# One transformer layer on one core: merges as seven products, units in pairs, the second MLP product by 1024 inner features, the output projection by token half, one pool throughout

## The chip, the cores and the metric

One core of one Trainium2 chip runs the whole layer in a single launch. Its engines are TensorE (PE; its weight loads are PEld), VectorE (DVE), ScalarE (ACT), GpSimd (POOL) and SyncE (SP), which issues nearly all DMAs. The metric is the time of one execution in device microseconds, the median of several.

## The reference

One layer over 1024 tokens of width 1024, with 256 context tokens, all in fp32:

```python
hx = modulate(rms_norm(x, norm1), sh1, sc1)                # and hc from ctx
ak, av, gk, gv, lrf, lrb, aq, gq, go, ga, gg = split(hx @ w_in)
attn = softmax(rope(qx) @ [kx, kc].T) @ [vx, vc]           # 8 query heads on 2 key/value heads
gla  = gated linear attention, both directions, 4 heads
y = sigmoid(ga) * (attn @ w_br_attn) + sigmoid(gg) * (gla @ w_br_gla)
x = x + gt1 * (y @ w_out)
x = x + gt2 * (square(relu(modulate(rms_norm(x, norm2), sh2, sc2) @ w_mlp1)) @ w_mlp2)
```

The weights of the two merges and of the output projection are 1024x1024, those of the MLP 1024x4096 and 4096x1024.

## The kernel before

Everything is kept feature-major: 128 features on the partitions, tokens along the free axis, in two halves of 512. Each fp32 operand is split into a rounded high part and a low part (`hilo`, `split`: a cast on ScalarE, a subtraction on VectorE), and every product of a 128x128 weight block with a 128x512 operand block is three matmuls (`mm3`, L167 to L169).

First come the input projections with the gated linear attention (to about 906 us), then softmax attention in 16 blocks of 4 heads x 128 queries, all queries of key/value head 0 and then all of head 1. The results of both branches go to DRAM as high and low parts (`glaT` L768, `atT` L1006). Both stages take their tiles from a pool `sp`, which is closed after attention. Then a second SBUF pool `tl` and a second PSUM pool are opened (L1407) for what follows:

- The merges (`merge_branches` L1137). `operand` loads all of a branch's output, 16 loads of 512 KB; `plain` (L1118) loads 256 columns of weights, splits them into four tiles and makes the four results of 128 features x 512 tokens, each of 8 products. `first` and `second` multiply by the gates.
- The output projection with the same `plain`, in chunks of 256 columns over both token halves. After the last chunk `norm2` normalises half 0, then half 1, and builds the operand blocks of the first MLP product.
- The first MLP product: 16 units of 256 inner features. Each is a 2x2 block product (two halves of the inputs x two column blocks x two token halves) made as seven products for eight (Strassen in Winograd's form): GpSimd makes four sums of weight blocks (`sums`), seven splits follow, and each of the seven results is added up in PSUM and on VectorE. The order is `ORDER` (L1252). The seven operand blocks `B[0..6]` are sums and differences of the normalised activations; only `B[0]` and `B[1]` come from token half 0 alone. The unit stores the seven blocks of its own output (`uD`).
- The second MLP product: 8 chunks of 512 inner features, two column halves each, again seven products; `load` (L1327) brings a block as a raw, a high and a low tile, and L1352 accumulates each result onto the residual in SBUF.

The framework sets the order. It takes the program as written, decides for each engine when an instruction would be ready in its own model of the chip, and lays down a fixed queue for each engine; of what is ready, what is written first goes first. Tiles of one tag are handed out in the order written and wait for a released slot. So a load can be moved forward only as far as a slot is free.

```python
1148:    for c in range(4):                        # merge: 4 chunks of 256 columns
1122:        for s, th in ((0, 0), (1, 0), (0, 1), (1, 1)):
1125:                self.product(p, w[s][h], lambda j: x(4 * h + j, th), 4, h == 0, h == 1, more=False)   # 4 of the 8 products of a result
1359:        for u in (0, 0, 1, 1):                # ahead of the other units:
1360:            next(units[u])                    # products 0 and 1 of two units
```

Of the kernel before, what the change touches and what calls it, by code (L numbers as in the profile page):

```python
# [32 lines left out]
NU, NW, NM = 31, 8, 9  # L33
# [34 lines left out]
class Layer:  # L68
    def __init__(self, ctx, tc, a, out, dbg=None):
        self.ctx, self.tc, self.nc, self.a, self.out = ctx, tc, tc.nc, a, out  # L70
        self.dbg = dbg or {}
        e = ctx.enter_context
        self.cp = e(tc.tile_pool(name="cp", bufs=1))
        self.dp = e(tc.tile_pool(name="dp", bufs=1, space=DRAM))
        self.n = 0

# [11 lines left out]
    def t(self, tag, shape, dt=F32, bufs=2):  # L88
        return self.sp.tile(list(shape), dt, tag=tag, name=self.nm(tag), bufs=bufs)
# [14 lines left out]
    def psum_phase(self, name, bufs):  # L104
        self.pbufs = bufs
        self.ptag = {}
        return self.tc.tile_pool(name=name, bufs=1, space=PSUM)
# [10 lines left out]
    def rsqrt(self, x, n):  # L118
# [8 lines left out]
        for _ in range(5):  # L127
# [617 lines left out]
    def proj_go(self, h):  # L745
# [3 lines left out]
        def g():  # L749
# [5 lines left out]
            def finish():  # L755
                tp, th = pend.pop()
                pt = self.ps("a")
                for f in range(2):
                    for i in range(2):
                        nc.tensor.transpose(pt[:, (2 * f + i) * P:(2 * f + i + 1) * P], th[:, i, f * P:(f + 1) * P], self.ident)  # L760
                for f in range(2):
                    if tp % 2 == 0:
                        gt[f] = (self.m2(F32R), self.m2(F32R))
                    hi, lo = (x[:, (tp % 2) * 256:(tp % 2 + 1) * 256] for x in gt[f])
                    src = pt[:, f * 256:(f + 1) * 256]
                    nc.scalar.activation(hi, src, AF.Copy, scale=self.gnh[:, f:f + 1])
                    nc.vector.scalar_tensor_tensor(lo, src, self.gnh[:, f:f + 1], hi.bitcast(F32), op0=ALU.mult, op1=ALU.subtract)
                    if tp % 2 == 1:  # L768
                        for j in range(2):
                            self.move(self.glaT[j][2 * h + f][:, (tp // 2) * 512:(tp // 2 + 1) * 512], gt[f][j])  # L770
# [15 lines left out]
        return (9, g)  # L786

# [130 lines left out]
    def q_load(self, kv, qb):  # L918
        q = [self.m2(F32R, (P, 4, P)) for _ in range(2)]
# [11 lines left out]
    def attention(self, tail, gate):  # L931

        nc = self.nc
        with self.psum_phase("pat", {"s": 2, "sc": 1, "b": 3}) as self.pp:
# [53 lines left out]
            def values(kv, qb, st, kt):  # L988
# [14 lines left out]
                at = self.S(F32R, (P, 2, 4, P))  # L1003
                self.hilo(at[:, 0], at[:, 1], rv)
                for j in range(2):
# [77 lines left out]
    def U(self, dt=F32R, shape=(P, 2, 512)):  # L1083
        return self.t("U", shape, dt, bufs=NU)

    def m(self, dt=F32, shape=(P, 512)):
        return self.t("m", shape, dt, bufs=NM)
# [7 lines left out]
    def split(self, v, engine=None):  # L1095

        w = self.t("W", (P, 2, 512), F32R, bufs=NW)
        hi, lo = w[:, 0, :], w[:, 1, :]
        if len(v.shape) == 3:
            hi, lo = (x.rearrange("p (a b) -> p a b", b=v.shape[2]) for x in (hi, lo))  # L1100
        elif len(v.shape) == 4:
            hi, lo = (x.rearrange("p (a b c) -> p a b c", b=v.shape[2], c=v.shape[3]) for x in (hi, lo))
        self.nc.scalar.copy(hi, v)  # L1103
        (engine or self.nc.vector).tensor_tensor(lo, v, hi.bitcast(F32), op=ALU.subtract)  # L1104
        return w

    def wcols(self, name, c0):
        return self.a[name][:, c0:c0 + 256].rearrange("(k p) c -> p k c", p=P)

    def product(self, out, w, x, n, first, last, at=lambda j: j * P, more=True):  # L1110

        for j in range(n):
            c = at(j)
            xh, xl = x(j)
# [125 lines left out]
    def plus(self, a, b, o, engine=None):  # L1240
        r = self.m()
        (engine or self.nc.vector).tensor_tensor(r, a, b, op=o)
        return r

# [205 lines left out]
```

## Time and profile before

| | |
|---|---|
| median of 3 runs | 2216.52 us (2214.68 to 2220.52) |
| the profiled execution | 2216.28 us, its span 2214.5 us |
| PE busy | 2038.4 us (92%), 12622 matmuls |
| DVE busy | 1492.8 us (67%) |
| ACT busy | 934.7 us (42%) |
| POOL busy | 449.5 us (20%) |
| DMA | 271.50 MB |

```profile
PE   5999898998989999999998599996899998889999
DVE  6533778669588487877776224438666666778997
POOL 2100322213131022100000000001222333433642
PEclk9999999998999999999999799997999998989999
```

Each digit is the busy share of one fortieth of the span (55.4 us), in tenths. TensorE is nearly always busy; its dents in the second half are slice 23 (1218 to 1273 us), slices 28 and 29 (1495 to 1606) and slices 34 to 36 (1827 to 1993). Matmuls overlap in time in the records, so their own durations (about 390 ns) add up to more than they take; the spacing of their starts is what counts.

### The profile page before, as it was taken

Reading aid. Unit: us, or ns where it says so; the run is one execution under the profiler, and the core shown is the slowest. Engines: PE = TensorE matmul, PEld = TensorE weight load, DVE = VectorE, ACT = ScalarE, POOL = GpSimd, SP = SyncE. Lnnn points to the kernel's source line nnn. Section 1 sums busy time; section 2 is a strip of 40 time slices with the busy share of each in tenths; the row PEclk is TensorE's granted clock in tenths of the full one; section 3 lists DMA queues with packets and bytes.
Section 4 is the critical chain, followed back from the end, with each engine's and each line's share of the span. In section 5 each row is a group of like instructions: output and inputs, shape, how many; then the busy total and the mean of one; then the engine's idle time right before and its main releaser. Section 6 shows DMA issues by size and latency. Waiting matters only on the chain.

```text
span 2214.5 us, 32247 instructions
## 1 busy us (share of the span) xinstructions
PE 2038.4 (92%) x12622; PEld 1718.3 (78%) x12622; DVE 1492.8 (67%) x2372; ACT 934.7 (42%) x1607; POOL 449.5 (20%) x272
## 2 busy tenths in 40 slices
PE   5999898998989999999998599996899998889999
PEld 2898687887878998788887488884688886667877
DVE  6533778669588487877776224438666666778997
ACT  3344544434254322566665111222655554323431
POOL 2100322213131022100000000001222333433642
PEclk9999999998999999999999799997999998989999
DMA  8143421232325333231222915320444446343433
GB/s 292 57 119 110 138 87 45 96 102 72 121 82 172 106 123 134 79 88 54 58 57 65 372 54 204 128 86 34 143 157 152 157 157 214 122 142 117 171 120 118
DMA packets 208696, 271.50 MB, mean 123 GB/s; under 512 B 16880, under 2 KB 144000, under 8 KB 208544
## 3 DMA queue, kind: packets, MB, share of 16 engines
q1 hardware_dynamic: 208480, 269.31, 36.4%
q8 instruction: 99, 1.62, 0.3%
q0 software_dynamic: 64, 0.13, 0.1%
q14 instruction: 53, 0.43, 0.1%
HBM read 191.79 MB, written 77.61 MB: 122 GB/s over the span
## 4 chain that ended last, share of the span: by engine, by line
PE 52%; DVE 12%; DMA 3%; issue 2%; ACT 1%; POOL 1%; SPq 0%; DVEq 0%; POOLq 0%; ACTq 0%
PE g L168 12%; PE g L169 12%; PE g L167 12%; PE b L973 3%; DVE U L1352 2%; PE b L167 2%; PE b L169 2%; PE b L168 2%; DVE W L1104 2%; DMA U<-u 2%; DVE G L848 1%; PE s L167 1%; PE s L169 1%; PE s L168 1%; DVE U L1332 1%
## 5 line engine op out<-in xcount | busy, mean ns | idle before, releaser
L167 PE MATMUL g<-U,W 128*128 128x512 f32 x1280 | 503.5, 397 | 60.7 <-ACT W L1103 30.6
L168 PE MATMUL g<-U,W 128*128 128x512 f32 x1280 | 508.2, 397 | 26.0 <-POOL U L1332 20.7
L169 PE MATMUL g<-U,W 128*128 128x512 f32 x1280 | 505.5, 396 | 0.0
L167 PEld LDWEIGHTS g<-U,W 128*128 128x128 f32 x1280 | 244.3, 191 | 120.5 <-ACT W L1103 34.5
L168 PEld LDWEIGHTS g<-U,W 128*128 128x128 f32 x1280 | 245.5, 192 | 83.1 <-POOL U L1332 23.7
L169 PEld LDWEIGHTS g<-U,W 128*128 128x128 f32 x1280 | 245.6, 192 | 51.7 <-DVE W L1104 0.2
L167 PE MATMUL g<-whi,S 128*128 128x256 f32 x896 | 261.8, 292 | 0.0
L168 PE MATMUL g<-wlo,S 128*128 128x256 f32 x896 | 256.0, 286 | 0.0
L169 PE MATMUL g<-whi,S 128*128 128x256 f32 x896 | 255.5, 285 | 0.0
L1262 POOL TENSOR_TENSOR Q<-R 128x512 f32<-128x512 f32 x32 | 43.0, 1342 | 954.8 <-DMA R<-in_w_mlp_dram 532.8
L1103 ACT CAST W<-R 128x512 fp32r<-128x512 f32 x144 | 89.0, 623 | 321.1 <-PE g L169 285.6
L1352 DVE SCALAR_TENSOR_TENSOR U<-g,mc,U 128x512 f32<-128x512 f32 x224 | 161.7, 742 | 49.8 <-PE g L169 49.6
L1104 DVE TENSOR_TENSOR W<-R,W 128x512 fp32r<-128x512 f32 x144 | 128.6, 897 | 66.4 <-ACT W L1103 65.1
L168 PEld LDWEIGHTS g<-wlo,S 128*128 128x128 f32 x896 | 171.6, 191 | 1.4 <-issue 0.4
L167 PEld LDWEIGHTS g<-whi,S 128*128 128x128 f32 x896 | 171.6, 191 | 1.4
L169 PEld LDWEIGHTS g<-whi,S 128*128 128x128 f32 x896 | 171.3, 191 | 0.3
L1104 DVE TENSOR_TENSOR W<-Q,W 128x512 fp32r<-128x512 f32 x128 | 112.4, 879 | 65.2 <-ACT W L1103 64.7
L167 PE MATMUL g<-S,whi 128*128 128x512 f32 x336 | 139.8, 416 | 5.1 <-ACT S L262 5.1
L1103 ACT CAST W<-Q 128x512 fp32r<-128x512 f32 x128 | 79.0, 621 | 146.3 <-PE g L169 114.3
L169 PE MATMUL g<-S,wlo 128*128 128x512 f32 x336 | 136.5, 406 | 0.0
L168 PE MATMUL g<-S,whi 128*128 128x512 f32 x336 | 135.8, 404 | 0.0
L155 POOL TENSOR_TENSOR wlo<-wraw,whi 128x1024 fp32r<-128x1024 f32 x32 | 89.9, 2827 | 224.3 <-ACT whi L154 221.0
(299 smaller groups left out, 3966.8 us busy)
## 6 DMA issues: line engine op xcount, KB each, us to landing
R<-in_w_mlp_dram SPq DMA_DIRECT2D x32, 1024.0 KB, 5.2
wraw<-in_w_in_dram SPq DMA_DIRECT2D x60, 512.0 KB, 4.3
u<-m SPq DMA_DIRECT2D x112, 256.0 KB, 3.3
U<-u SPq DMA_DIRECT2D x56, 512.0 KB, 6.8
m<-in_w_ada_dram SPq DMA_DIRECT2D x64, 256.0 KB, 4.4
G<-in_w_ada_dram SPq DMA_DIRECT2D x16, 512.0 KB, 10.5
S<-in_xT_dram SPq DMA_DIRECT2D x8, 512.0 KB, 9.8
wraw<-in_w_in_dram SPq DMA_DIRECT2D x16, 256.0 KB, 3.4
```

The source lines that it names most:

```text
L155: self.lo_engine.tensor_tensor(lo[:, s, :], raw, hi[:, s, :].bitcast(F32), op=ALU.subtract)
L167: nc.tensor.matmul(out, lh, rh, start=first, stop=False, skip_group_check=more)
L168: nc.tensor.matmul(out, lh, rl, start=False, stop=False, skip_group_check=more)
L169: nc.tensor.matmul(out, ll, rh, start=False, stop=last, skip_group_check=more)
L848: nc.vector.tensor_tensor(uv[:, :, :, s, :], xv[:, :, :, 1 - s, :], tv[:, :, :, s, :], op=ALU.mult)
L973: nc.tensor.transpose(pt[:, h * P:(h + 1) * P], src, self.ident)
L1103: self.nc.scalar.copy(hi, v)
L1104: (engine or self.nc.vector).tensor_tensor(lo, v, hi.bitcast(F32), op=ALU.subtract)
L1262: tt(s[0], a21, a22, op=ALU.add)
L1332: (nc.gpsimd if i in (2, 3, 6) else nc.vector).tensor_tensor(lo, raw, hi.bitcast(F32), op=ALU.subtract)
L1352: nc.vector.scalar_tensor_tensor(d, p, self.mc[:, 3, b:b + 1], d, op0=ALU.mult, op1=ALU.add)
```

## The change

The merges become units of the same kind as in the MLP: 4 units of 256 columns in each merge, seven products each (`unit`, `merge_unit`); the branch outputs are stored as the seven operand blocks (`glaD`, `atD`), whose differences GpSimd makes (`operands`). Attention runs its blocks in groups of four (both key/value heads, queries q and q + 4), so that a group's four results make one set of operand blocks. Units run in pairs, one product of each in turn (`pair`), and during a pair the blocks for the next stage are loaded step by step (`load_blocks`). The output projection takes the token halves one after the other, with the weights loaded twice. The first MLP product opens with products 0 and 1 of four units. The second goes by 1024 inner features and 256 columns. The pool `sp` stays open to the end: its 19 + 16 tiles of 4 KB hold the operand blocks, the gates, the results and the residual; the weight tiles (`R`, `W`, six in place of eight) take the place of the input projection's weights once these are done. The reciprocal root takes three Newton steps in place of five.

```diff
-        for _ in range(5):
+        for _ in range(3):
...
+                th_ = tp // 2
                 for f in range(2):
...
-                    nc.scalar.activation(hi, src, AF.Copy, scale=self.gnh[:, f:f + 1])
-                    nc.vector.scalar_tensor_tensor(lo, src, self.gnh[:, f:f + 1], hi.bitcast(F32), op0=ALU.mult, op1=ALU.subtract)
...
+                        gt[f, th_] = self.m2()
+                    nc.scalar.activation(gt[f, th_][:, (tp % 2) * 256:(tp % 2 + 1) * 256], pt[:, f * 256:(f + 1) * 256], AF.Copy, scale=self.gnh[:, f:f + 1])
+                if tp % 2 == 1:
+                    self.operands(gt, th_, lambda i: self.glaD[h, i])
...
+    def operands(self, b, th, dst, view=lambda t: t):
+        nc = self.nc
+        tt = nc.gpsimd.tensor_tensor
+        put = lambda i, t: nc.sync.dma_start(dst(i), view(t))
+        if th == 0:
+            put(0, b[0, 0])
+            put(1, b[1, 0])
+            return
+        put(2, b[1, 1])
+        tt(b[0, 0], b[0, 1], b[0, 0], op=ALU.subtract)
+        put(4, b[0, 0])
+        tt(b[0, 1], b[1, 1], b[0, 1], op=ALU.subtract)
+        put(6, b[0, 1])
+        tt(b[1, 1], b[1, 1], b[0, 0], op=ALU.subtract)
+        put(5, b[1, 1])
+        tt(b[1, 0], b[1, 0], b[1, 1], op=ALU.subtract)
+        put(3, b[1, 0])
...
-        q = [self.m2(F32R, (P, 4, P)) for _ in range(2)]
+        t = self.S(F32R, (P, 2, 4, P))
+        q = [t[:, j] for j in range(2)]
...
-                at = self.S(F32R, (P, 2, 4, P))
-                self.hilo(at[:, 0], at[:, 1], rv)
-                for j in range(2):
-                    self.move(self.atT[j][4 * kv:4 * kv + 4, :, qb * P:(qb + 1) * P].rearrange("h d t -> d h t"), at[:, j])
-            blocks = [(kv, qb) for kv in range(2) for qb in range(NT)]
+                th = qb // 4
+                self.at[kv, th] = rb
+                if kv == 1:
+                    if th == 0:
+                        return
+                    t0 = qb % 4 * P
+                    for t in range(2):
+                        self.operands(self.at, t, lambda i: self.atD[:, i, :, t0:t0 + P].rearrange("j d t -> d j t"), lambda r: r.rearrange("p (h t) -> p h t", t=P))
+            blocks = [(kv, q + 4 * th) for q in range(4) for kv in range(2) for th in range(2)]
+            self.at = {}
...
-            self.lo_engine = nc.gpsimd
+            self.close_wts.close()
+            self.wts, self.close_wts = self.open("tw", side="right", reuse_waits="tile")
             late = []
             for n, (kv, qb) in enumerate(blocks):
                 nxt, sg = None, iter(())
-                if n == 4:
+                if n == 0:
                     kvs[1] = self.kv_load(1)
+                if n in (9, 11):
+                    self.load_blocks(self.glaD, n // 11)
                 if n + 1 < len(blocks):
...
+        w = self.t("W", (P, 2, 512), F32R, bufs=6)
+        hi, lo = (w[:, i, :].rearrange("p (a b) -> p a b", b=P) for i in range(2))
...
+    ORDER = (0, 1, 5, 4, 6, 2, 3)
+    def four(self, i):
+        return (self.S if i in (0, 1, 5) else self.G)(F32R, (P, 2, 512))
+    def split_block(self, b, v, engine=None):
+        self.nc.scalar.copy(b[:, 0, :], v)
+        (engine or self.nc.vector).tensor_tensor(b[:, 1, :], v, b[:, 0, :].bitcast(F32), op=ALU.subtract)
+    def load_block(self, b, src, engine=None):
+        v = b[:, 1, :].bitcast(F32)
+        self.nc.sync.dma_start(v, src)
+        self.split_block(b, v, engine)
+        return b
+    def load_blocks(self, src, i):
+        for j in range(4):
+            self.nB[i, j] = self.load_block(self.four(i), src[j, i], self.nc.gpsimd if j % 2 else None)
...
+    def unit(self, src, sink, halves=True):
+        B = self.B
+        raw = self.raw_weights(src)
+        blk = (lambda kh, s: raw[:, kh::2, s * P:(s + 1) * P]) if halves else (lambda kh, s: raw[:, 4 * kh:4 * kh + 4, s * P:(s + 1) * P])
+        A, w, bank = {0: blk(0, 0), 1: blk(1, 0)}, {}, {}
+        for i in self.ORDER:
+            wi = w.pop(i) if i in w else self.split(A[i])
+            if i in (0, 1, 4):
+                bank[i] = self.ps("p" if i == 0 else "g")
+            p = bank[{1: 1, 4: 4, 2: 4}.get(i, 0)]
+            self.product(p, wi, lambda j: B[i, j], i in (0, 1, 4), True)
+            if i == 1:
+                A[4], A[5], A[6], A[2] = self.sums(blk)
+                w[3] = self.split(blk(1, 1))
+            sink(i, p)
+            yield
+    def pair(self, a, b, also=None):
+        for i in self.ORDER:
+            next(a)
+            next(b)
+            if also:
+                also(i)
...
+        def store(k):
+            return lambda b, th, v: nc.sync.dma_start(self.yD[k][b][:, th * 512:(th + 1) * 512], v)
+        for i in self.ORDER[2:]:
+            self.load_blocks(self.glaD, i)
+        self.B, self.nB = self.nB, {}
+        u = lambda c: self.merge_unit("w_br_gla", c, 1, store(0))
+        self.pair(u(0), u(1))
+        self.pair(u(2), u(3), lambda i: self.load_blocks(self.atD, i))
+        self.B, self.nB = self.nB, {}
+        self.Y = Y = {}
+        u = lambda c, last: self.merge_unit("w_br_attn", c, 0, last)
+        self.pair(u(0, store(1)), u(1, store(1)))
+        def keep(b, th, v):
+            Y[b, th] = (self.G if th else self.S)(F32R, (P, 2, 512))
+            self.split_block(Y[b, th], v)
+        def also(i):
+            if i in (0, 4):
+                th = i // 4
+                for b in range(4):
+                    Y[b, th] = self.load_block((self.G if th else self.S)(F32R, (P, 2, 512)), self.yD[1][b][:, th * 512:(th + 1) * 512], nc.gpsimd if b % 2 else None)
+        self.pair(u(2, keep), u(3, keep), also)
...
+        self.B = {}
+        Z = {}
+        for th in range(2):
+            ssq = self.m()
...
+                bank = [self.ps("p") for _ in range(4)]
+                for kh in range(2):
+                    raw = self.raw_weights(self.a["w_out"][kh * 512:(kh + 1) * 512, c * 512:(c + 1) * 512].rearrange("(k p) c -> p k c", p=P))
+                    for i in range(4):
+                        w = self.split(raw[:, :, i * P:(i + 1) * P])
+                        self.product(bank[i], w, lambda j: self.Y[4 * kh + j, th], kh == 0, kh == 1, more=False)
+                        if kh == 0:
+                            continue
+                        b = 4 * c + i
+                        v = Z[th, i % 2, c][:, i // 2, :]
+                        nc.vector.scalar_tensor_tensor(v, bank[i], mc[:, 0, b:b + 1], v, op0=ALU.mult, op1=ALU.add)
...
+            self.norm2(th, ssq, lambda t, e, j: Z[t, e, j // 2][:, j % 2, :])
...
+        for j in range(4):
+            norm(0, j)
+            norm(1, j)
+            tt(z(0, 0, j), z(1, 0, j), z(0, 0, j), op=ALU.subtract)
+            tt(T2(j), z(1, 1, j), z(0, 0, j), op=ALU.subtract)
+            self.block(5, j, T2(j))
...
+            b = 2 * q + s
+            d = x[b][th]
+            nc.vector.scalar_tensor_tensor(d, p, self.mc[:, 3, b:b + 1], d, op0=ALU.mult, op1=ALU.add)
+        return self.unit(self.wcols("w_mlp2", q * 256, n * D), sink)
...
-        for u in (0, 0, 1, 1):
+        for u in (0, 1, 0, 1, 2, 3, 2, 3):
             next(units[u])
-        for g in units:
-            run_all(g)
+        for u in (0, 2):
+            for _ in range(5):
+                next(units[u])
+                next(units[u + 1])
+        for u in range(4, 14, 2):
+            self.pair(units[u], units[u + 1])
+        self.nB = {}
+        load = lambda n: lambda i: self.load_blocks(self.uD[4 * n:4 * n + 4], i)
+        self.pair(units[14], units[15], load(0))
...
+        for n in range(4):
+            self.B, self.nB = self.nB, {}
+            self.pair(self.mlp2_unit(n, 0, x), self.mlp2_unit(n, 1, x))
+            self.pair(self.mlp2_unit(n, 2, x), self.mlp2_unit(n, 3, x), load(n + 1) if n < 3 else None)
...
-        with self.tc.tile_pool(name="sp", bufs=2) as self.sp:
-            self.small_constants()
-            self.attention(*self.in_projection())
-        with self.tc.tile_pool(name="tl", bufs=2, reuse_waits="tile") as self.sp, self.psum_phase("pout", {"g": 6, "a": 2}) as self.pp:
+        self.sp, close_sp = self.open("sp")
+        self.mid, close_mid = self.open("mid")
+        self.wts, self.close_wts = self.open("wts", side="right")
+        self.small_constants()
+        self.attention(*self.in_projection())
+        close_mid.close()
+        self.mid, close_mid = self.open("tm", reuse_waits="tile")
+        with self.psum_phase("pout", {"p": 4, "g": 2, "a": 2}, "tile") as self.pp:
             self.load_mod()
             self.merge_branches()
             self.out_projection()
             self.mlp()
```

## Rows read from the trace of the kernel before

**Rows 1.** Stretches: us, PE, PEld, DVE, ACT, POOL busy (x instructions), clock, DMA, GB/s.
```profile
906.00:1211.00 305.00, 304.47 (x1756) 248.70 (x1754) 231.48 (x469) 208.72 (x444) 1.05 (x1) 1.00 0.23 66
1211.00:1240.80 29.80, 0.00 (x0) 0.00 (x0) 1.38 (x2) 1.26 (x3) 0.00 (x0) 0.55 0.95 359
1240.80:1506.50 265.70, 265.43 (x1165) 218.78 (x1165) 103.97 (x170) 53.64 (x89) 5.09 (x4) 0.99 0.40 143
1506.50:1566.00 59.50, 28.12 (x92) 20.78 (x93) 53.26 (x101) 21.34 (x38) 6.46 (x5) 0.68 0.13 42
1566.00:1852.00 286.00, 286.00 (x1261) 236.23 (x1261) 172.75 (x212) 163.99 (x277) 90.41 (x63) 1.00 0.47 166
1852.00:2211.00 359.00, 325.49 (x1348) 259.66 (x1347) 306.05 (x366) 119.73 (x164) 150.10 (x82) 0.95 0.39 136
```
**Rows 2.** Timeline of TensorE near the end: start, duration, what.
```profile
2201.06 0.39 PE L167 MATMUL g<-U,W 128*128 128x512 f32 x1
...
2210.36 0.39 PE L169 MATMUL g<-U,W 128*128 128x512 f32 x1
```
**Rows 3.** Timeline from attention to the merges; in brackets the idle time before.
```profile
1210.61 0.39 PE L169 MATMUL b<-G,S 128*128 128x512 f32 x1
...
1228.13 0.38 SPq L1092 DMA_DIRECT2D R<-in_w_br_gla_dram  x1
...
1240.16 1.14 ACT L1103 CAST W<-R 128x512 fp32r<-128x512 f32 x2 [27.78 <-DMA R<-in_w_br_gla_dram]
```
**Rows 4.** Timeline of the second half's normalisation.
```profile
1518.12 0.74 DVE L1191 SCALAR_TENSOR_TENSOR U<-g,mc,U 128x512 f32<-128x512 f32 x1
...
1530.35 1.09 PE L366 MATMUL a<-ident,ty 128*128 128x128 f32 x4 [7.97 <-DVE ty L130]
...
1532.10 1.29 DVE L1218 TENSOR_TENSOR U<-U,m 128x512 f32<-128x512 f32 x2 [1.89 <-ACT m L1215]
...
1541.96 1.22 PE L167 MATMUL g<-U,W 128*128 128x512 f32 x2 [10.52 <-ACT U L184]
```
**Rows 5.** Waits of TensorE, 1205 to 2215 us: total, times, longest.
```profile
PE g L167 <- ACT W L1103: 30.6, 2, 29.8
PE g L168 <- POOL U L1332: 20.7, 7, 5.8
```
**Rows 6.** DMA issues of the operand blocks: count, KB each, median us to landing.
```profile
U<-u SPq DMA_DIRECT2D x56, 512.0 KB, 6.8
```
**Rows 7.** Groups by line and shape, 1566 to 1852 us (first MLP product).
```profile
L1104 DVE TENSOR_TENSOR W<-Q,W 128x512 fp32r<-128x512 f32 x60 | 41.5, 692 | 64.2 <-ACT W L1103 63.6
L1104 DVE TENSOR_TENSOR W<-R,W 128x512 fp32r<-128x512 f32 x45 | 39.7, 882 | 0.3 <-ACT W L1103 0.3
...
L1263 POOL TENSOR_TENSOR Q<-Q,R 128x512 f32<-128x512 f32 x16 | 28.0, 1747 | 0.0
...
L1264 POOL TENSOR_TENSOR Q<-R 128x512 f32<-128x512 f32 x16 | 20.8, 1300 | 0.0
```
**Rows 8.** The same view, 1241 to 1418 us (merges).
```profile
L1104 DVE TENSOR_TENSOR W<-R,W 128x512 fp32r<-128x512 f32 x39 | 26.5, 691 | 58.1 <-ACT W L1103 58.0
L1103 ACT CAST W<-R 128x512 fp32r<-128x512 f32 x39 | 23.8, 622 | 136.3 <-PE g L169 132.8 <-DMA R<-in_w_br_gla_dram 3.3
```
**Rows 9.** The same view, 1852 to 2211 us (second MLP product).
```profile
L1352 DVE SCALAR_TENSOR_TENSOR U<-g,mc,U 128x512 f32<-128x512 f32 x224 | 161.7, 742 | 49.8 <-PE g L169 49.6
...
L1104 DVE TENSOR_TENSOR W<-Q,W 128x512 fp32r<-128x512 f32 x60 | 65.5, 1092 | 1.0 <-ACT W L1103 1.0
L1332 POOL TENSOR_TENSOR U<-U,U 128x1024 fp32r<-128x1024 f32 x24 | 62.0, 2589 | 59.2 <-ACT U L1331 59.2
...
L1104 DVE TENSOR_TENSOR W<-R,W 128x512 fp32r<-128x512 f32 x46 | 53.3, 1162 | 0.0
```
**Rows 10.** The same view, 0 to 880 us, VectorE (output of the gated linear attention).
```profile
L767 DVE SCALAR_TENSOR_TENSOR m<-a,gnh,m 128x256 fp32r<-128x256 f32 x32 | 15.3, 479 | 12.5 <-ACT m L766 12.2
```
**Rows 11.** Costliest groups of the whole execution: the casts of weights.
```profile
L1103 ACT CAST W<-R 128x512 fp32r<-128x512 f32 x144 | 89.0, 623 | 321.1 <-PE g L169 285.6
```

More of the change, by code (lines that the diff above doesn't have):

```diff
@@ L1093, in raw_weights, with split @@
         return raw
[L1095 to L1102, printed above, removed]
+    def split(self, v):
+        w = self.t("W", (P, 2, 512), F32R, bufs=6)
+        hi, lo = (w[:, i, :].rearrange("p (a b) -> p a b", b=P) for i in range(2))
@@ L1103, in split @@
         self.nc.scalar.copy(hi, v)
-        (engine or self.nc.vector).tensor_tensor(lo, v, hi.bitcast(F32), op=ALU.subtract)
+        self.nc.vector.tensor_tensor(lo, v, hi.bitcast(F32), op=ALU.subtract)
         return w
[L1107 to L1114, printed above, removed]
-            self.mm3(out, w[:, 0, c:c + P], w[:, 1, c:c + P], xh, xl, first and j == 0, last and j == n - 1, more and not first)
@@ new lines, in product @@
+    def product(self, out, w, x, first, last, more=True):
+        for j in range(4):
+            c, b = j * P, x(j)
+            self.mm3(out, w[:, 0, c:c + P], w[:, 1, c:c + P], b[:, 0, :], b[:, 1, :], first and j == 0, last and j == 3, more and not first)
+    ORDER = (0, 1, 5, 4, 6, 2, 3)
[4 more added lines that the diff above has]
+        (engine or self.nc.vector).tensor_tensor(b[:, 1, :], v, b[:, 0, :].bitcast(F32), op=ALU.subtract)
@@ L1211, in norm2, with block @@
+    def block(self, i, j, v, engine=None):
+        self.B[i, j] = self.four(i)
+        self.split_block(self.B[i, j], v, engine)
+    def norm2(self, th, ssq, z):
         nc, mc = self.nc, self.mc
@@ L1284, in store @@
[L1284 to L1298 removed]
+        tt = nc.vector.tensor_tensor
@@ new lines, in mlp1_unit, with put, act, sink @@
+        X = {}
+        def put(i, v):
+            nc.sync.dma_start(self.uD[u, i], v)
+        def act(v, src, p=None):
+            if p is not None:
+                tt(v, v, p, op=ALU.add)
+            nc.scalar.activation(v, src, AF.Relu)
+            nc.scalar.activation(v, v, AF.Square)
+        def sink(i, p):
+            if i == 0:
+                X[1] = self.S(F32, (P, 2, 512))
+            elif i == 4:
+                X[2] = self.S(F32, (P, 2, 512))
+            x11, x12 = X[1][:, 0, :], X[1][:, 1, :]
+            x22, x21 = (X[2][:, 0, :], X[2][:, 1, :]) if 2 in X else (None, None)
+            if i == 0:
+                nc.scalar.copy(x11, p)
@@ L1299, in mlp1_unit @@
             elif i == 1:
-                done(11, self.plus(keep[11], p, ALU.add))
-                store(0, out[11])
+                act(x11, x11, p)
+                put(0, x11)
             elif i == 5:
-                keep[12] = copied(p)
+                nc.scalar.copy(x12, p)
             elif i == 4:
-                keep[22] = copied(p)
+                nc.scalar.copy(x22, p)
             elif i == 6:
-                done(22, self.plus(keep[22], p, ALU.add))
-                store(2, out[22])
+                act(x22, x22, p)
```

307 lines of the change are left out of this document (126 added, 181 removed).

## The prediction

> **What bounds the kernel now.** I read three views in this order: the busy time of each engine by stage, then who made TensorE wait, then the timeline at each gap. The stage table shows [rows 1] that attention (906 to 1211 us) and the first MLP product (1566 to 1852) keep TensorE busy without a hole, while three stretches do not: 1211 to 1240.8 has no matmul at all, 1506.5 to 1566 has 92, and the second MLP product has 1348 in 359 us. In the last 9.3 us two matmuls 41 places apart start at 2201.06 and 2210.36 [rows 2]: 0.2268 us for each 128x512 matmul at full clock. With that price the table reads as lost time. Stretch 1211 to 1240.8 loses 29.8. Stretch 1506.5 to 1566 loses 59.5 - 92 x 0.2268 = 38.6. The second MLP product loses 359 - 1348 x 0.2268 = 53.3. Merges and output projection lose 265.7 - 1165 x 0.2268 = 1.5, the first MLP product nothing. So the part after attention is 3840 matmuls x 0.2268 = 870.9 us plus about 129 us of the rest: 121.7 of holes, the others being small matmuls of the normalisation and the clock after a hole, and 3.7 us from the last matmul to the end.
>
> What makes the holes: at the start, SyncE issues the 16 loads of the first merge's operand ahead of the first weights; attention's last matmul starts at 1210.61, the weights are issued at 1228.13 and the cast of them begins at 1240.16 [rows 3]. At 1506 to 1566 TensorE has a few products of two units as cover and then waits for the second normalisation, 7.97 us ahead of the transposes and 10.52 for the first new operand block [rows 4]. In the second MLP product it waits for the low parts of the loaded blocks, 20.7 us behind GpSimd alone [rows 5]; those blocks need three tiles each, so the loads run late (6.8 us to landing [rows 6]), and VectorE is busy 306 of 359 us [rows 1].
>
> **The change part by part.** The sum starts from the profiled execution: span 2214.5, time 2216.28, so 1.8 around it; the median of the runs shown is 2216.52, the same within 0.3 us.
>
> *Merges as seven products.* Before: 2 merges x 4 chunks x 32 products x 3 = 768 matmuls. After: 2 x 4 units x 7 x 4 products x 3 = 672. Minus 96, or 21.8 us, on the path, since TensorE is the bound there (rates in [rows 1]). The rest of the 3744 matmuls stays: output projection 384, each MLP product 1344. 3744 x 0.2268 = 849.1 us. This is the surest term.
>
> *What the seven products add.* Weight sums on GpSimd, four a unit, each between 1.30 and 1.75 us [rows 7], some 6 us a unit, where GpSimd had next to no work (5 us in 266 [rows 1]); 56 loads of 256 KB with cast and subtraction in place of the old 32 loads of 512 KB; partial results kept and added on VectorE. A pair of units lasts 168 x 0.2268 = 38.1 us. VectorE in the busiest merge pair (loading the next operand): 14 weight splits, 14 block splits, and per unit 3 adds, 4 multiplications. At the price without GpSimd, 0.69 [rows 8], that is 28 x 0.69 + 14 x 0.69 = 29 us; at the price it has when GpSimd is busy, 1.09 to 1.16 [rows 9], for those with both inputs in SBUF, 28 x 1.12 + 8 x 0.69 + 6 x 1.12 = 44. So between 0 and 6 us are lost in such a pair, more where gates are added: 0 to 23 over the four pairs. I take 5, because only a part of the time has GpSimd at work: the first MLP product, which has the same sums, shows 0.69 and 0.88 mixed [rows 7].
>
> *One pool throughout, loads ahead.* The operand blocks 0 and 1 are loaded during attention blocks 9 and 11, the weight ring is opened as soon as the last input projection is done, and PSUM is handed over tile by tile. So the first 4 products of the pair (10.9 us) have everything when attention ends, and block 5 can take the three to four free tiles during the last attention block. What follows needs 16 blocks of 256 KB, 4 MB; the hole of before carries 359 GB/s [rows 1], so 12 us, begun as the last score tiles come free, against 16.3 us of cover with block 5. The hole of 29.8 falls to between 0 and 29.8; I take 1. If the loads come only when attention has let go of its tiles, the cover ends first and the hole is the old one.
>
> *Attention and what lies before it.* Attention stays at TensorE's pace. Both head groups are loaded at once, the queries move into the big tiles, 16 casts and subtractions go, 16 GpSimd sums and 8 block splits come; all beside a TensorE that is busy 304.5 of 305 us [rows 1]. A cast that stands ahead of attention's own casts and waits for its DMA holds ScalarE some 3 us. The first query tile now holds one of the 19 tiles that the last gate needs, so that gate waits for the first scores. I put -2 to +10 here. Before attention 32 operations of 0.48 us leave VectorE [rows 10] and each reciprocal root loses 6 small operations; the output operand waits for 16 GpSimd sums that nobody waits for. I put -10 to 0. Together -12 to +10, taken as -2.
>
> *Output projection by token half.* The normalisation of half 0 now lies beside 192 matmuls (43.5 us) of half 1: hidden. That of half 1 is exposed, with 8 products (21.8 us) of four units as cover instead of 4. Working: the chain from the last product to the row on all partitions took 1518.12 to 1532.1, 14 us [rows 4]; without 6 of 18 small operations about 12. Then each of four blocks costs VectorE five operations, 3.3 us, and the first needs ScalarE twice in between: first block at 16, last at 26, and some 10 us of weight splits and adds lie on VectorE in the same stretch, so up to 36. TensorE comes for the last block at 24: a wait of 2 to 12. The other end is the hole of now less the added cover, 38.6 - 10.9 = 27. I take 8.
>
> *Second MLP product by 1024.* The VectorE accumulations fall from 224 to 112, at 0.742 [rows 9] 83 us less; blocks are loaded half a chunk (38 us) ahead into tiles that have just come free, against 6.8 us to landing, and each block takes one tile instead of three. VectorE per pair: 14 x 1.12 + 14 x 0.742 = 26 us, with loads up to 42, mean at most 34 of 38.1. So TensorE is the bound, and of 53.3 us between 0 and 53.3 stay; I take 8, with the change from the first product to the second in it, where the residual tiles are loaded last.
>
> *Small rest.* First MLP product 1, the small matmuls of half 0's normalisation 3, clock after a hole 1: where TensorE had stood still 10.5 us it ran at half its clock for some 5 us (granted clock 0.68 in that stretch [rows 1]), and shorter waits should cost less.
>
> Sum: 1211.0 - 2 + 1 + 849.1 + 5 + 8 + 8 + 5 + 3.7 = 2088.8; with 1.8 around it 2090.6, say **2091 us**, 5.7% less.
>
> *A rule that speaks against it.* A weight split takes 0.691 us where GpSimd is idle and 1.09 to 1.16 where it works 150 of 359 us [rows 1, 8, 9]. The Trainium skill ("SBUF — State Buffer", Who interferes with whom) says that a VectorE operation with two SBUF inputs and a GpSimd operation that reads SBUF exclude each other for the whole instruction. By it the two engines' times in the second MLP product would add; that is rival B. The trace agrees as far as it goes: the split of raw weights in the first MLP product, which meets the sums, takes 0.882, and that of the sums 0.692 [rows 7].
>
> **The rivals.**
> *A, the hole at the start stays.* The loads of blocks 4, 6, 2, 3 need tiles that attention holds to its end. For it: ScalarE waited 27.8 us for the loads and the weights behind them [rows 3]. Against: half the bytes are wanted, the weights come early. Time 2091 + 29 = 2120.
> *B, VectorE and GpSimd get in each other's way.* GpSimd works 16 units x 6 + 56 x 1.3 (half of the 2.59 for the double width [rows 9]) = 169 us in the second MLP product, VectorE 168 operations of 0.69 with two SBUF inputs (116 us) and 83 us of accumulations: 368 if nothing overlaps, 305 if the accumulations hide. I price it with the loss of now staying whole, 45 us more than I took (inside the 63 that 368 would cost), and the merges losing 23 instead of 5. Time 2091 + 45 + 18 = 2154.
> *C, slower: the ring of weight slots.* It shrinks from 8 to 6, and two slots in a pair (four at the start of the first MLP product) hold the last weights from the second step on, so four move. If a split could start only when the product before its own has ended, each of 56 + 32 + 224 = 312 products would wait for cast and subtraction, 0.62 + 0.69 = 1.3 us [rows 8]: 406 us, time 2497. It decides from 125/312 = 0.40 us a product. For it: the casts' idle time ends on TensorE, 285.6 us [rows 11], so the ring is already what holds them. Against: they run that far ahead, TensorE waited for weights 30.6 us in all, 29.8 of it at the start [rows 5], and four slots are 10.9 us of products against 1.3.
>
> **How the numbers follow.** Forecast 0.70, its own range 2061 to 2114 (all best ends at once, -12 up to attention's end, 0 at the start, in the merges and in the second product, 2 after the output projection, give 2061). A 0.13, B 0.10, C 0.04, anything else 0.03. All worst ends at once would give 2214, which needs every cover to fail; the range goes from 2056 (5 us more for small matmuls that hide) to one large term staying, 2138. A measurement of this kernel can tell 0.3% (6.6 us) from no change: its three runs lie 5.8 us apart. Faster 0.94 (forecast, A, B and most of the rest), the same 0.02, slower 0.04.
>
> **What would show it.** Right: the first merge matmul within 3 us of attention's last; 672 matmuls in the merges in some 155 us; one short wait after the output projection, below 15 us, with at most a brief loss of clock; the second MLP product in 305 to 320 us with VectorE below nine tenths. Wrong: weight casts behind the block loads at 1211 (A); splits over 1.1 us and VectorE above 95% (B); TensorE waiting for W in every product (C); attention longer than 310 us.

## The result and the profile after

The changed kernel takes 2158.4 us (median; 2154.2 to 2160.3), the kernel before 2218.5 beside it: ratio 0.9725, interval 0.9699 to 0.9751. That is 60 us less, where 125 were forecast; 2158 lies above the range. The profiled execution has a span of 2152.3. One execution of all the runs below was slow, the profiled one of *e10b_stores* (2493 us at a granted clock of 0.75): it is left out of that run's time, and its trace is not read.

Stretches of the changed kernel, columns as in [rows 1]: the passage into attention, attention, merges and output projection, the normalisation of half 1, the two MLP products.

```profile
850.00:950.00 100.00, 79.16 (x417) 63.55 (x416) 61.26 (x116) 41.60 (x87) 11.27 (x9) 0.93 0.61 182
950.00:1214.80 264.80, 264.63 (x1528) 219.45 (x1526) 196.34 (x401) 178.26 (x384) 21.96 (x17) 1.00 0.16 48
1214.80:1490.80 276.00, 262.80 (x1105) 207.80 (x1104) 202.67 (x266) 115.98 (x204) 108.14 (x69) 0.98 0.64 215
1490.80:1527.50 36.70, 14.02 (x53) 10.85 (x52) 34.09 (x42) 23.94 (x40) 13.06 (x8) 0.67 0.08 29
1527.50:1844.10 316.60, 307.73 (x1318) 247.16 (x1316) 189.50 (x236) 177.46 (x308) 117.06 (x78) 0.99 0.49 164
1844.10:2148.10 304.00, 303.96 (x1296) 244.51 (x1296) 223.25 (x255) 110.37 (x186) 151.90 (x99) 0.99 0.43 143
```

The second MLP product is now without a hole, and still 1296 recorded matmuls fill 304 us, 10 more than they would at the price of [rows 2]. The timeline near the end shows why: these two are 40 places apart, 9.33 us, so 0.2333 us each, where [rows 2] has 0.2268.

```profile
2138.54 0.40 PE L174 MATMUL g<-G,W 128*128 128x512 f32 x1
...
2147.87 0.40 PE L175 MATMUL p<-G,W 128*128 128x512 f32 x1
```

The timeline where [rows 3, 4] had the two large holes, and at the passage between the MLP products. The first merge product now stands right behind attention, but two waits follow; at the normalisation TensorE waits once, for 22.68 us.

```profile
1214.56 0.40 PE L175 MATMUL b<-G,S 128*128 128x512 f32 x1
1214.80 0.39 PE L173 MATMUL p<-S,W 128*128 128x512 f32 x1
...
1522.59 0.76 PE L173 MATMUL g<-S,W 128*128 128x512 f32 x1 [22.68 <-DVE S L1382]
...
1835.20 0.50 PE L175 MATMUL g<-S,W 128*128 128x512 f32 x1 [2.57 <-DVE W L1128]
...
1844.14 0.76 PE L173 MATMUL p<-S,W 128*128 128x512 f32 x1 [6.35 <-DVE S L1431]
```

The longest waits of TensorE from 1150 us on, in the columns of [rows 5] (total, times, longest): L1382 is the addition that frees a PSUM bank, L1431 the accumulation of the second product, L1127 and L1128 cast and subtraction of weights.

```profile
PE g L173 <- DVE S L1382: 22.7, 1, 22.7
PE p L173 <- DVE S L1431: 6.3, 1, 6.3
PE g L175 <- DVE W L1128: 6.1, 2, 3.6
PE p L173 <- ACT W L1127: 3.4, 1, 3.4
PE g L173 <- ACT W L1127: 3.1, 1, 3.1
```

*The account.* From the first merge matmul (1214.80) to the last (2147.87) are 933.3 us with its own length; 3744 x 0.2333 are 873.6. What successive starts lie further apart than that, summed by place, is the loss there, the slow clock behind a wait included (e1 to e9 are experiments below; two of their expectations put the start of the merges at 13.2 and 12.6, which this way of counting makes 12.2 and 11.6):

| | forecast | after | e1 | e3 | e6 | e9 |
|---|---|---|---|---|---|---|
| us for a 128x512 matmul | 0.2268 | 0.2333 | 0.2267 | 0.2333 | 0.2267 | 0.2267 |
| start of the merges | 1 | 11.7 | 12.3 | 12.1 | 12.2 | 11.6 |
| rest of merges | 5 | 8.2 | 10.6 | 10.1 | 11.6 | 10.9 |
| normalisation, half 1 | 8 | 25.4 | 26.1 | 10.9 | 12.9 | 11.6 |
| into the second MLP product | 8 | 10.8 | 15.1 | 13.3 | 14.7 | 6.8 |
| first merge matmul at | 1209 | 1214.8 | 1219.9 | 1220.8 | 1208.8 | 1211.6 |

Against the forecast's 2088.8 the changed kernel has more: matmuls 24.5, merges 13.9, normalisation 17.4, passage 2.8, end of attention 5.8, rest -0.9; together 63.5, the whole difference. (The instruction orders of after and e3 are the same up to the merges, yet the first merge matmul comes at 1214.8 and 1220.8: single spans are read to 6 us, the losses by place more closely.)

### The profile page after: what moved, and what is told of

Its sections match the earlier page's. It is cut to its first block, busy times and chain, and to the rows that moved or that the text cites. A ratio compares the mean times of both kernels' runs of the same rounds, so it can differ in the third digit from the quotient of the medians.

```text
span 2152.3 us, 32698 instructions
## 1 busy us (share of the span) xinstructions
PE 2016.5 (94%) x12526; PEld 1688.3 (78%) x12526; DVE 1482.9 (69%) x2216; ACT 1002.8 (47%) x1783; POOL 632.1 (29%) x408
## 4 chain that ended last, share of the span: by engine, by line
PE 47%; DVE 5%; DMA 4%; issue 2%; ACT 1%; POOL 0%; SPq 0%; DVEq 0%; ACTq 0%; POOLq 0%
PE p L173 7%; PE p L175 7%; PE p L174 7%; PE g L173 4%; PE g L175 4%; PE g L174 4%; PE b L996 3%; PE b L173 2%; PE b L175 2%; PE b L174 2%; PE s L173 2%; PE s L174 1%; PE s L175 1%; DVE G L1155 1%; DMA S<-y 1%
## 5 line engine op out<-in xcount | busy, mean ns | idle before, releaser
L1128 DVE TENSOR_TENSOR W<-Q,W 128x512 fp32r<-128x512 f32 x160 | 131.1, 824 | 96.1 <-ACT W L1127 95.8
L173 PE MATMUL p<-S,W 128*128 128x512 f32 x384 | 155.1, 404 | 11.6 <-DVE S L1431 6.3
L1127 ACT CAST W<-R 128x512 fp32r<-128x512 f32 x152 | 93.9, 620 | 151.1 <-PE p L175 106.4
L1128 DVE TENSOR_TENSOR W<-R,W 128x512 fp32r<-128x512 f32 x152 | 138.2, 914 | 24.2 <-ACT W L1127 24.2
L1175 POOL TENSOR_TENSOR Q<-R 128x512 f32<-128x512 f32 x40 | 59.9, 1497 | 323.2 <-DVE W L1128 225.4
L175 PE MATMUL p<-S,W 128*128 128x512 f32 x384 | 154.2, 402 | 0.2 <-DVE W L1128 0.2
L174 PE MATMUL p<-S,W 128*128 128x512 f32 x384 | 154.2, 402 | 0.0
L1127 ACT CAST W<-Q 128x512 fp32r<-128x512 f32 x160 | 98.6, 621 | 118.3 <-PE g L175 53.3
L174 PE MATMUL p<-G,W 128*128 128x512 f32 x384 | 152.0, 396 | 0.0
L173 PE MATMUL p<-G,W 128*128 128x512 f32 x384 | 151.9, 395 | 0.0
L175 PE MATMUL p<-G,W 128*128 128x512 f32 x384 | 151.9, 395 | 0.0
L191 DVE TENSOR_TENSOR G<-b,G 128x512 fp32r<-128x512 f32 x164 | 111.8, 686 | 48.0 <-ACT G L190 47.8
## 6 DMA issues: line engine op xcount, KB each, us to landing
G<-in_w_ada_dram SPq DMA_DIRECT2D x16, 512.0 KB, 10.6
```

Source lines behind the costliest of these rows:

```text
L173: nc.tensor.matmul(out, lh, rh, start=first, stop=False, skip_group_check=more)
L174: nc.tensor.matmul(out, lh, rl, start=False, stop=False, skip_group_check=more)
L175: nc.tensor.matmul(out, ll, rh, start=False, stop=last, skip_group_check=more)
L191: self.nc.vector.tensor_tensor(lo, src, hi.bitcast(F32), op=ALU.subtract)
L1128: self.nc.vector.tensor_tensor(lo, v, hi.bitcast(F32), op=ALU.subtract)
L1175: tt(s[0], a21, a22, op=ALU.add)
```

## The experiments

**The price of a matmul.** A product has two operands in SBUF: the weights, and the moving tile that streams past them. The address of the weight tiles W (read from the built programs; traces hold none) was the one thing that I found to differ for every product of the part after attention: 192 past a multiple of 256 bytes before, 224 after; the moving tiles (U, then S and G) start 192 past one in both. *e1_pad32*, from the changed kernel:

```diff
+        pad = self.pad.tile([P, 8], F32, name="pad", bufs=1)   # own pool, right side, under "wts"/"tw"
```

> The changed kernel with a dead tile of 32 bytes a partition under the pool of the weight tiles, so that each weight tile W starts 32 bytes lower (at a multiple of 64 bytes, 448 past a multiple of 512, where it was 480 past); nothing else. Theory 1 (where the weights lie in SBUF sets the pace): the matmuls after attention start every 0.2267 us again, as in the kernel before, instead of every 0.2333; 3744 x 0.0066 = 24.7 us less, so 2134 us, ratio 0.9886 to the changed kernel. Rival (the slower pace comes from how two products alternate, or from what the other engines do): spacing stays 0.2333 and the time 2158, within 6 us.

2141.7 us, 0.9657 (0.9634 to 0.9680) of before. Theory 1 holds in the pace, 0.2267; of the 24.7 us about 8 went into longer waits at four places (table). *e2_before_w32* does the reverse to the kernel before:

```diff
+            self.shift = self.t("shift", (P, 8), bufs=1)   # ahead of the first W
```

> The kernel before, with a dead tile of 32 bytes a partition ahead of its weight tiles, so that W starts 32 bytes higher (32 past a multiple of 64). Theory 1 (place of the weights): its matmuls after attention go from one every 0.2267 us to one every 0.2333: 3840 x 0.0066 = 25 us more where TensorE is the bound, 2244 us, ratio 1.011 to the kernel before (less where a wait hides it). Rival (pace set by the alternation of products): 0.2267 and 2218 stay, ratio 1.000.

2234.4 us, 1.0072 (1.0053 to 1.0091), and 0.2333: the pace is as forecast, the time 16 of the 25 us. Then which places are good? *p160* and *p224* are e1 with 40 and 56 numbers in the dead tile.

> The changed kernel with a dead tile of 160 bytes: weight tiles at 64 past a multiple of 256 (64 past a multiple of 64: 0). If a start at a multiple of 64 bytes is all that counts: one matmul every 0.2267 us, 2141. If 256 counts (the fast ones so far all start 192 past a multiple of 256, like the moving tiles; the head's weights in the kernel before start 64 past one and were slow): 0.2333, 2158.

2160.7 us.

> The changed kernel with a dead tile of 224 bytes: weight tiles at a multiple of 256 (and of 64). If a multiple of 64 is all that counts: 0.2267 and 2141. If the weights must lie in another 128-byte half than they do here, or in step with the moving tiles (192 past a multiple of 256): 0.2333 and 2158.

2160.2 us. Both slow (0.2324 and 0.2333), so a multiple of 64 is not it. The last two move the moving tiles, on top of e6 (below, fast with weights and moving tiles both at 192), by a dead tile of 32 bytes in the first pool; *m224w224* leaves out e1's dead tile, so that its weights are at 224 again:

> All three edits (e6_three), with the operand tiles S and G (the moving ones) 32 bytes higher, 224 past a multiple of 256; the weight tiles stay at 192 past one. If the place of the weight tiles alone counts: one matmul every 0.2267 us and 2123. If weights and moving tiles must start at the same place of 256 bytes, or the moving tiles at a multiple of 64: 0.2333 and some 17 us more, 2140.

2136.9 us: slow, with the weights where they were fast.

> As m224w192, but without the dead tile under the weights: operand tiles and weight tiles both at 224 past a multiple of 256. If equal places are what counts: 0.2267 and 2123. If 192 counts for the weights: 0.2333 and 2140.

2121.4 us: fast. Matmuls between 1600 and 1650 us, the same view (second group: PE busy and its count) of before, e2, after, e1, p224, m224w192, m224w224 in this order:

```profile
1600.00:1650.00 50.00, 50.00 (x222) 41.42 (x221) 32.76 (x40) 28.85 (x49) 17.66 (x12) 1.00 0.47 164
```
```profile
1600.00:1650.00 50.00, 50.00 (x216) 40.27 (x215) 26.58 (x35) 27.06 (x47) 13.91 (x10) 1.00 0.38 135
```
```profile
1600.00:1650.00 50.00, 50.00 (x216) 40.24 (x215) 24.04 (x33) 26.14 (x45) 12.52 (x9) 1.00 0.37 126
```
```profile
1600.00:1650.00 50.00, 50.00 (x222) 41.40 (x222) 23.75 (x34) 27.00 (x47) 14.09 (x10) 1.00 0.38 131
```
```profile
1600.00:1650.00 50.00, 50.00 (x216) 40.30 (x215) 24.83 (x34) 27.12 (x46) 11.82 (x8) 1.00 0.42 146
```
```profile
1600.00:1650.00 50.00, 50.00 (x216) 40.13 (x216) 29.15 (x41) 27.80 (x48) 13.16 (x9) 1.00 0.48 160
```
```profile
1600.00:1650.00 50.00, 50.00 (x223) 41.38 (x222) 27.86 (x41) 27.84 (x49) 11.80 (x8) 1.00 0.56 191
```

222, 216, 216, 222, 216, 216, 223, all at full clock. In these seven, and p160, a product is fast where weights and moving tile start the same distance past a multiple of 256 bytes, slow where they differ (by 32, 64, 128 or 224). The input projection bears it out in tiles of its own, whose weights each dead tile on the right side moved too: the middle spacing there is 0.227 in e1, e6, e9 and m224w224, where the starts agree, and 0.232 to 0.234 in the others.

**The cover of the normalisation.** *e3_order* writes the same work in another order: `norm2` becomes a generator.

```diff
-            self.norm2(th, ssq, lambda ...)
+            self.n2 = self.norm2(th, ssq, lambda ...)   # yields after its row of factors and after each block
+            next(self.n2)
...
             for _ in range(5):
+                if u == 0:
+                    next(self.n2)
                 next(units[u])
```

> The changed kernel, with the second half's normalisation written in pieces: first its row of factors, then the 8 covering products of four units, then block 5, product 5 of two units, block 4, product 4 and so on. Same work, other order. Theory 2 (the cover broke because the additions that free PSUM banks and the weight splits stood behind the whole normalisation in VectorE's queue): the single wait of 22.7 us falls below 8, the half clock behind it goes, some 18 us less: 2140, ratio 0.992 to the changed kernel. Rival (VectorE's 30 us of normalisation bound this stage in any order): the wait only moves to the first new block, 15 us or more, and the time is 2152 or more, ratio above 0.997.

2148.6 us, 0.9681 (0.9667 to 0.9696). The 22.7 us are gone; the two longest waits left in the stage are these, and the loss there fell by 14.5 us. At other places 4.8 came back (table), and the time lies between theory 2's 2140 and its rival's 2152.

```profile
1519.66 0.76 PE L173 MATMUL p<-S,W 128*128 128x512 f32 x1 [3.14 <-ACT W L1127]
...
1524.41 0.79 PE L175 MATMUL p<-S,W 128*128 128x512 f32 x1 [3.57 <-DVE W L1128]
```

*e5_banks* asks which half of theory 2 it is, the bank or the queue:

```diff
-        with self.psum_phase("pout", {"p": 4, "g": 2, "a": 2}, "tile") as self.pp:
+        with self.psum_phase("pout", {"p": 4, "g": 4}, "tile") as self.pp:
+            self.ptag = {"a": "g"}
```

> The changed kernel with 4 banks for the side results in place of 2 (the small sums of the normalisation share them), the order as it was. Theory 2a (the third unit's side product waits only for a bank): TensorE goes on for the 2 products that were blocked and the rest of one, some 8 us, then waits for what stands behind the normalisation in VectorE's queue, about 14 us: 2150. Theory 2b (the queue alone: weight splits and additions): the wait stays 20 us or more, 2156 to 2160.

2159.6 us. The wait for the bank is gone and a wait of 14.48 for a weight subtraction in its place, as 2a had it; but a weight cast now costs 6.90 more, the stage loses 26.0, and the time is the one that 2b named. The bank was the first thing late, VectorE's queue the price. In VectorE's timeline of the changed kernel the additions (L1382) and weight splits follow the last of the block subtractions:

```profile
1512.88 6.56 DVE L1155 TENSOR_TENSOR G<-G,G 128x512 fp32r<-128x512 f32 x9
1519.36 2.48 DVE L1155 TENSOR_TENSOR G<-S,G 128x512 fp32r<-128x512 f32 x4
1521.77 1.27 DVE L1382 TENSOR_TENSOR S<-S,g 128x512 f32<-128x512 f32 x2
```

**The start of attention.** *e4_q0*:

```diff
+        if kv == qb == 0:
+            q = [self.m2(F32R, (P, 4, P)) for _ in range(2)]
+        else: ...
```

> The changed kernel, with the query tile of the first attention block in two of the small tiles (as before the change) instead of one of the 19 big ones. Theory 3 (that tile is what the last gate lacks, so gate and first scores wait for each other): the gate's first tanh comes at about 870 instead of 893.8, TensorE's busy share in 875 to 925 rises from 0.65 to 0.9, attention ends 8 to 12 us sooner: 2148, ratio 0.995. Rival (the keys, values and queries that are fetched ahead of need hold up the start): the end of attention moves by less than 3 us, 2156 to 2160.

2150.4 us, 0.9691 (0.9677 to 0.9706), 8 less than the changed kernel, whose four runs all lie above these four: theory 3 holds. The first merge matmul starts at 1207.4, and the gate's first activation (ScalarE's timeline, changed kernel and then e4) at 865 instead of 894. TensorE's busy share in 875 to 925 rose from 0.65 to 0.78 only, not to 0.9.

```profile
893.79 1.08 ACT L602 ACTIVATE S<-b 128x512 f32<-128x512 f32 x2
```
```profile
865.33 0.60 ACT L602 ACTIVATE S<-b 128x512 f32<-128x512 f32 x1 [7.01 <-PE b L175]
```

**All three.** *e6_three* has e1, e3 and e4.

> The changed kernel with all three edits at once: weight tiles 32 bytes lower, the normalisation of half 1 in pieces between the covering products, the first query tile in small tiles. If the three causes are separate, their gains add: 2158.4 - 17 - 10 - 8 = 2123, ratio 0.957 to the kernel before. Rival (a faster TensorE runs into VectorE and the weight loads, as the 7 us that the place of the weights gave less than its 24.7 suggest): 2133 or more.

2122.8 us, 0.9573 (0.9557 to 0.9589). The three gains add: 2158.4 - 16.7 - 9.8 - 8.0 would be 2123.9.

**What is left at the start of the merges and at the passage.** *e7_dve*, on e6:

```diff
-            ... src[j, i], self.nc.gpsimd if j % 2 else None)
+            ... src[j, i])
```

> All three edits (e6_three) and one more: the subtractions of the operand blocks that are loaded for merges and second MLP product all go to VectorE; GpSimd, which had every second one, keeps only the sums of weight blocks. Theory 4 (at the start of the merges the weights wait for GpSimd's sums, which stand behind block subtractions there, and with both engines at work VectorE's operations take 1.78 us instead of 0.68): of the 13.2 us lost at the start of the merges 6 to 8 come back, of the 14.7 at the start of the second MLP product 3 to 6, VectorE's busy time in the rest falls or stays: 2112, ratio 0.995 to e6_three. Rival (VectorE is the scarcer engine, 42 to 45 of 50 us busy where blocks are loaded): 14 more operations of 0.68 a pair make it the bound there, 2125 or more.

2125.9 us, 0.9579 (0.9557 to 0.9602), no difference from e6. Theory 4 falls: 12.2 us are lost at the start as before, 12.7 at the passage, and 9.8 more inside the second product. *e8_sum1*, on e6, gives `sums` an engine:

```diff
+        return self.unit(..., which == 1, nc.vector if which == 1 and c == 0 else None)
```

> All three edits (e6_three), and the four weight sums of the very first merge unit are made on VectorE (idle for some 7 us there) instead of GpSimd, which keeps the second unit's. Theory 5 (at the start TensorE waits for the sums, which can begin only when attention's small tiles are free and then stand behind attention's last sums and block subtractions on GpSimd): of the two waits there (3.7 and 3.0 us, with the loss of clock behind them 13.2) at least half goes: 2116, ratio 0.997 to e6_three. Rival (the blocks themselves come late, each 256 KB load landing behind the other): the waits stay, now for blocks: 2121 to 2125.

2120.7 us, 0.9562 (0.9544 to 0.9580), no difference from e6, so theory 5's gain did not come. The traces show its wait and what took its place. In the changed kernel ScalarE's two late weight casts wait last for GpSimd's sums (L1176):

```profile
1228.89 0.62 ACT L1127 CAST W<-Q 128x512 fp32r<-128x512 f32 x1 [1.33 <-POOL Q L1176]
...
1235.17 0.62 ACT L1127 CAST W<-Q 128x512 fp32r<-128x512 f32 x1 [4.62 <-POOL Q L1176]
```

In e8 the first of these casts stands right behind casts of blocks that waited for their load, and comes no sooner after the first merge matmul (14 us in both); instead of the second wait TensorE has one of 4.7 us for a weight subtraction on VectorE.

```profile
1228.02 1.31 ACT L1157 CAST G<-G 128x512 fp32r<-128x512 f32 x2 [5.10 <-DMA G<-gla]
1229.24 0.61 ACT L1130 CAST W<-Q 128x512 fp32r<-128x512 f32 x1
```

*e9_x*, on e8 (the other 13 residual tiles are loaded in another order too):

```diff
+        for k in ((0, 0), (2, 0), (0, 1)):          # before the last pair of the first product
+            x[k] = self.m()
+            nc.sync.dma_start(x[k], self.xD[k[0]][:, k[1] * 512:(k[1] + 1) * 512])
```

> As e8_sum1, and the first three residual half tiles of the second MLP product are loaded before the last pair of the first into three small tiles that lie idle. Theory 6 (the passage waits for the residual, which is loaded behind everything else: 4.7 us): that wait goes, 4 to 5 us less than e8_sum1. Rival (the wait passes to the next late thing, the weight splits that take 1.78 us beside GpSimd's sums, or to the next residual tiles): less than 2 us.

2111.5 us, 0.9518 (0.9502 to 0.9533), the fastest of all. Theory 6: the wait is gone, and with the clock that fell behind it 7 us of the passage. The time fell by 9.2, more than the 4 to 5 forecast; 3.6 us of the gain between the two profiles lie ahead of the merges, in code that e9 leaves as it was, and are not counted as its doing. For the start, SyncE's timeline of the changed kernel suggested the next theory: 5 of 16 block loads, then stores of attention (L795) that wait for its last results, 2 loads, 2 stores, 9 loads.

```profile
1204.90 3.71 SPq L1160 DMA_DIRECT2D G<-gla  x5
1215.72 2.12 SPq L795 DMA_DIRECT2D at<-m  x2
1217.94 0.94 SPq L1160 DMA_DIRECT2D G<-gla  x2
1222.12 1.74 SPq L795 DMA_DIRECT2D at<-m  x2
1223.95 4.29 SPq L1160 DMA_DIRECT2D G<-gla  x9
```

*e10_stores*, on e9: `operands` issues the last pair's stores with `nc.gpsimd.dma_start`. *e10b_stores*: the same without e8's edit.

> As e9_x, and the seven stores of attention's last pair of blocks are issued by GpSimd, which makes what they store, instead of SyncE. Theory 7 (the start of the merges waits for operand blocks whose loads stand behind these stores in SyncE's queue, and ScalarE's weight casts stand behind the casts of those blocks): the 16 loads are issued without a pause, the blocks come 5 to 6 us sooner, and of the 12.6 us lost at the start 5 or more come back: 2106, ratio 0.9975 to e9_x. Rival (the weight splits that stand behind 16 block splits on ScalarE and VectorE set the start): less than 2 us, 2110 to 2113.

2120.8 us, 0.9557 (0.9538 to 0.9577): 9 more than e9. The loads ran without a pause from 1200.4 to 1213.3, as theory 7 had it, but neither its gain nor its rival's 2110 to 2113 came: six block subtractions on VectorE, 0.68 us each when undisturbed, took 13.21:

```profile
1213.57 13.21 DVE L1158 TENSOR_TENSOR G<-G 128x512 fp32r<-128x512 f32 x6
```

GpSimd computed for 9.0 us in that time; 6 x 0.68 + 9.0 = 13.1: the two engines' times added. TensorE waited 10.4 us for a weight whose sum stood behind these; the start lost 17.4 us in place of 11.6, the rest of the merges 15.2 in place of 10.9. Whether early loads alone would help, as theory 7 says, is not shown.

> As e10_stores, but the weight sums of the first merge unit are back on GpSimd. If the sums do not matter (as e8_sum1 said): within 2 us of e10_stores. If they become the limit once the loads are early: 3 to 6 us more than e10_stores.

2126.3 us in its four executions, 0.9589 (0.9572 to 0.9606): between 5 and 6 more with the sums on GpSimd, the intervals just overlapping, so once the loads are early the sums seem to count. What the start of the merges would cost with early loads and an idle GpSimd wasn't tried.

## Why the prediction was wrong

- **3744 x 0.2268, called the surest term: failed, 24.5 us.** The count was right. The price came from a kernel whose weights and moving tiles happened to lie in step, and the change moved the weights into another pool. e1, e2 and the four after them show it. The sign was there to see: the products of the input projection, with their weights in other tiles, started 0.232 to 0.233 us apart already in the kernel before.
- **Normalisation of half 1, 8 taken of 2 to 27: the cover failed, 17.4 us.** The 25.4 lost is near the bad end of the term. I counted 8 products as cover; the wait came after little more than 5. The third unit's side product needed a bank whose addition stood behind 30 us of VectorE's work. I had put those additions and splits into VectorE's sum (up to 36 us), but not asked which of them TensorE needs first (e3, e5).
- **The start hole, 1 taken of 0 to 29.8, and 5 for the merges: 13.9 short.** The old hole did go: 0.24 us between attention and merges, rival A is out. The term counted blocks and asked whether they land in time. It left out that product 5, the third of a unit, needs weights that GpSimd has to sum first: in the changed kernel ScalarE waits for those sums 1.33 us ahead of the first late cast and 4.62 ahead of the second. With the first unit's sums taken off GpSimd (e8) late block loads and VectorE's queue keep the loss at 11.6. Which order would remove it isn't settled.
- **Attention, -2 of -12 to +10: 5.8 short.** The last query store was 13.6 us early (859.46 against 873.05). The edit that I named, the query tile in the gate's slot, took that back: I priced it inside +10, and e4 gave 8 us.
- **The second product and the passage, 8 of 0 to 53.3: right in kind.** 10.8 at the passage, nothing after: TensorE is busy 303.96 of 304. Landing of the blocks fell from 6.8 to some 3.5 us, at half the size (256 KB). The late residual that the term named is there (e9).
- **Rival B** is seen and doesn't decide: subtractions of loaded blocks take 1780 ns in the second product for the 24 that VectorE has in G tiles, 805 for the 18 in S tiles, and splits of raw weights 1065, as [rows 9] had 1162, yet VectorE is busy 223 of 304. **C** is out: weights held TensorE up 12.6 us in all.
- **The range** ended where one large term stayed. Four terms missed at once, all upwards, and in none was a count of operations wrong: the price, the cover and what a stage waits for were.

The Trainium skill ("SBUF — State Buffer", Who interferes with whom) has a VectorE operation with two SBUF inputs and a GpSimd operation that reads SBUF exclude each other; the 13.21 us of e10 agree.

## What to carry to other kernels

Before a matmul's price is carried over a change of pools, compare the start of its two SBUF operands: a dead tile of 32 bytes was worth 17 us here. A cover is counted by what the covering work needs from the covered engine's queue (a bank, a split), not by its length; written between the pieces that it covers, it lost 10.9 us here in place of 25.4. What is loaded last for the next stage belongs ahead of the last stage's work, into whatever small tiles lie idle.

## What the runs showed of the hardware

- In the products after attention a float32r matmul of 512 columns starts 0.2267 us after the last where weights and moving tile start equally far past a multiple of 256 bytes, 0.2333 where they lie 32, 64 or 224 apart, at a granted clock of 1.00 in both: by these figures 16 cycles at 2.4 GHz. Where they lie 128 apart it is 0.2324 (p160), and 0.2326 on average in the input projection of the kernel before. In attention the scores of the changed kernel, both operands at 192, were still 0.231 to 0.232 apart; why, stays open, and so does whether it is the relation itself or a finer pattern that it stands for.
- Six VectorE subtractions took 13.21 us beside GpSimd for the 4.1 that they take alone.
- Behind the waits of 3.4, 3.1 and 22.7 us in the changed kernel some matmuls started 0.43 us apart, the pace of 512 columns at 1.2 GHz, and were 0.63 long instead of 0.40 (granted clock 0.62 from 1238 to 1245 us, 1.00 in the 10 us after), so the wait of 22.7 cost 25.4 and the two of 3.4 and 3.1 cost 11.7 with what stood behind them.
